# Layer 1 of a two-layer mixer: modulation sums rest until a row pass ends, one norm and the first attention scores come one unit later

## The chip, the core and the metric

The kernel runs on one NeuronCore of a Trainium2 chip, as one launch. The metric is device time in microseconds (us), the median of repeated runs. A NeuronCore has engines that each work through their own list of instructions: TensorE (PE in the profile) multiplies, ScalarE (ACT) applies functions and copies, VectorE (DVE) does elementwise work and sums, GpSimd (POOL) does a small power function here, and SyncE (SP) issues the loads.

## The reference, cut to what matters

Two layers act on 256 latent and 256 context tokens of width 2048, in float32. Each layer is

```
shift, scale, gate = split(silu(c) @ w_mod + b_mod)
h    = rms_norm(x) * (1 + scale) + shift
u, v_sgu, za, q, k, v, zb = split(h @ w_in)        # D_IN = 5632
attn = softmax(rope(norm(q)) . rope(norm(k))) . v  # 8 heads of 128, 2 key/value heads
sgu  = gelu(u) * (w_sgu . norm(gelu(v_sgu)) + b_sgu)
x    = x + gate * (concat(sgu * silu(za), attn * silu(zb)) @ w_out)
```

In layer 1, the last one, the context gives only keys and values, so that q, u, v_sgu, za and zb are computed for 256 tokens and the 8 heads have two blocks of 128 queries each: 16 score blocks against 512 keys.

## The kernel before, in words

Every float32 operand is split into a high part `hi` and a rest `lo`, and a product is three matmuls: hi.hi, hi.lo, lo.hi (`three`, lines 334 to 336).

Most weights come through a `Stream`. The weights of a *job* (512 columns, for example "U0" or "ZA0") are eight *pieces* of 256 rows. For a piece, SP loads `raw`, ACT writes `hi` (line 200) and DVE writes `lo` (line 203). Three buffers hold `hi` and three hold `lo`; when the matmuls of piece n are about to be written down, the split of piece n+2 is written down first, and it takes the buffers that piece n-1 leaves. A piece of layer 1 is two *units* of twelve matmuls with 256 columns (six with 512 columns in jobs of kind "tok"). A job collects in four PSUM tiles of a ring of four (`acc`; two in "tok" jobs); after the last piece ACT applies gelu or silu to each (`act`, line 640, or `s`, line 663), which frees the tile for the next job.

The order on PE, SP, DVE and ACT is the order in which the Python program writes instructions down. After each unit the program calls `tick()`, which lets every waiting generator task advance if its countdown is over. So a `yield n` in a task means "n units later", and moving a task by one unit moves its instructions past whatever else is written down in that unit, on every engine. The tasks that matter here are:

- `next_task` prepares layer 1's rows: `hm` (DVE, line 722), `h` high (ACT, line 723), `h` rest (DVE, line 724) for 16 slices, first for latents, then for context. It sets `hold[0]`, and while that is set `mod_task` waits.
- `mod_task` computes modulation vectors on DVE, one `junk` instruction at a time (line 278, 128x1024).
- `sgu_v` evaluates gelu on a tile (line 663) and starts `head_norm`, whose first step is four sums of squares on ACT (`sq`, line 436).
- `attention_task` works through the heads. For head j: at its first step the scores `s` (PE), their maximum `nmx` (DVE, line 529) and the exponentials `p` (ACT, line 532); one unit later, on PE, the values `o` and the query transposes `qt` (each every second head) and the transposes `tp` of the head before; two units later the evacuations `qT` and `pt` (ACT line 470, then DVE line 471), a reciprocal (DVE, line 631) and the scaling of `p` (ACT, line 632); then, one unit later, the next head. In layer 1 that is four units, or two pieces, per head, called a *round* below.

Of the kernel before, what the change touches and what calls it, by code (L numbers as in the profile page):

```python
# [40 lines left out]
REST = (2, 0)  # L41
SGU_LAG = {4: 15, 2: 6}
CTX_WAIT = (15, 15)
HOLD_KT = 14
PAIRED = 2
NEXT_PACE = (1, 2)
MIX_LAG = 3
# [2 lines left out]
SGU_GAP = {4: 2, 2: 3}  # L50
# [12 lines left out]
def mixer_kernel(ctx: ExitStack, tc: tile.TileContext, a, out):  # L63
# [23 lines left out]
    def big(shape, dt=F32, s="big"):  # L87
        return u8.tile(shape, dt, tag="u8", name=nm(s))
# [4 lines left out]
    def misc(s="ms"):  # L93
        return msp.tile([P, 512], F32, tag="ms", name=nm(s))
# [4 lines left out]
    def small(shape, tag, dt=F32, bufs=None):  # L99
        kw = {} if bufs is None else {"bufs": bufs}  # L100
        return sp.tile(shape, dt, tag=tag, name=nm(tag), **kw)

    def t2(shape, s, dt=F32):
        return sp.tile(shape, dt, tag="t2", name=nm(s), bufs=NT2)

    def view(ap, pat, **kw):
        return ap.rearrange(pat, **kw)
# [197 lines left out]
    def spawn(gen, wait=0):  # L305
        tasks.append([gen, wait])
# [69 lines left out]
    hold = [False]  # L376
# [44 lines left out]
    def rstd_of(ss, n, mean_n):  # L421
        r = small([P, 4], "rs", bufs=12)[:, :n]
        V.tensor_scalar(out=r, in0=ss, scalar1=1.0 / mean_n, scalar2=EPS, op0=ALU.mult, op1=ALU.add)  # L423
        G.tensor_tensor(out=r, in0=r, in1=nhalf[:, :n], op=ALU.pow)  # L424
        return r

    def bc_last(ap, n, w):
        return view(ap, "p (h o) -> p h o", o=1).broadcast_to([P, n, w])

    def head_norm(q, n, kind):  # L430

        sq = t2([P, 512], "sq")[:, :n * HD]
        ss = small([P, 4], "ss", bufs=12)[:, :n]
        if kind in ACT_SUM:
            for h in range(n):
                S.activation(sq[:, h * HD:(h + 1) * HD], q[:, h, :], AF.Square, accum_out=ss[:, h:h + 1])
            yield NORM_PACE[0]
        else:
            S.activation(view(sq, "p (h d) -> p h d", h=n), q, AF.Square)
            yield NORM_PACE[0]  # L440
            V.tensor_reduce(out=ss, in_=view(sq, "p (h d) -> p h d", h=n), axis=AX.X, op=ALU.add)
        r = rstd_of(ss, n, HD)
        yield NORM_PACE[1]
        if kind in ACT_NORM:
            for h in range(n):
                S.activation(q[:, h, :], q[:, h, :], AF.Copy, scale=r[:, h:h + 1])
        else:
            V.tensor_tensor(out=q, in0=q, in1=bc_last(r, n, HD), op=ALU.mult)
# [20 lines left out]
    def evac_split(hi, lo, ps):  # L469
        S.copy(hi, ps)  # L470
        V.tensor_tensor(out=lo, in0=ps, in1=hi.bitcast(F32), op=ALU.subtract)

    def attention_task(L, kv, qa, units, done):
# [87 lines left out]
        rest = REST[L["l"]]  # L561
# [2 lines left out]
        ps, qT = turn_queries(*pairs[0])  # L564
        yield 1
        evac_split(qT[0], qT[1], view(ps[:, :256], "p (h d) -> p h d", h=2))
        yield rest + 1
        hold[0] = False
        paces = HEAD_PACE[L["l"]]
        n = len(heads)  # L570
# [88 lines left out]
    def sgu_v(L, buf, hf, nt):  # L659

        def f(tt, ps):
            b = buf[:, tt]
            S.activation(b, view(ps, "p (g d) -> p g d", g=4), AF.Gelu_apprx_tanh)  # L663
            spawn(head_norm(b, 4, "s"), SGU_GAP[nt] * tt)
        return f

    def sgu_consts(l, hf):
# [27 lines left out]
    def rows_diag(p1, nt):  # L695
        r = rstd_of(p1[:, :nt], nt, D)
        dg = t2([P, 512], "dg")
        for t in range(nt):
            V.tensor_scalar(out=dg[:, t * P:(t + 1) * P], in0=ident, scalar1=r[:, t:t + 1], scalar2=None,
                            op0=ALU.mult)  # L700
        return dg

    def rows_bc(dg, nt):
        pb = misc("rsb")
        for t in range(nt):
            ts = slice(t * P, (t + 1) * P)
            T.matmul(pb[:, ts], ones, dg[:, ts], start=True, stop=True)
        return pb[:, :nt * P]
# [9 lines left out]
    def modulate(L, kt, stream, xs, rb, hi, lo):  # L718

        sl = slice(stream, stream + 1)  # L720
        t_ = t2([P, 512], "hm")[:, :xs.shape[-1]]
        V.scalar_tensor_tensor(out=t_, in0=xs, scalar=L["A"][:, kt, sl], in1=rb, op0=ALU.mult, op1=ALU.mult)
        S.activation(hi, t_, AF.Identity, bias=L["B"][:, kt, sl])  # L723
        return lambda: V.scalar_tensor_tensor(out=lo, in0=t_, scalar=L["B"][:, kt, sl], in1=hi.bitcast(F32),
                                              op0=ALU.add, op1=ALU.subtract)
# [188 lines left out]
    def run_groups():  # L914
        first_pair()
        for gi in range(2, len(GROUPS)):
# [3 lines left out]
            for u in range(3 * NT):  # L920
                if u in LOADS:
                    load_w(p + 1, LOADS.index(u))
                if nxt and u in WAVE[0]:
                    mod_step(gi + 1, WAVE[0].index(u))
                if nxt and u == WAVE[1]:
                    nxt.finish()
                    make = rows_h(gi + 1)
                if make and u >= WAVE[2]:
                    make.pop(0)()
                if u in MOD_LOADS:  # L930
                    mod_load(gi + 2, MOD_LOADS.index(u) // 2)
                if u in SPLITS:
                    i = SPLITS.index(u)
                    split_w(p + (i > 0), (2, 0, 1)[i])
                if not nxt:
                    if u == 1:
                        st.load_to(4)
                    if u in (5, 9):
                        st.split_to(u // 4)
                    if u == ATT_AT:  # L940
                        spawn(attention_task(L0, kv0, qa0, [(hf, tt) for hf in range(2) for tt in range(NT)], done0))
                group_unit(p, *divmod(u, NT))
                tick()
# [68 lines left out]
    def sq_row(kt, s, xs):  # L1012
        later(0, lambda: later(0, add_square(sums1[0][:, s], xs, kt == 0)))
# [48 lines left out]
    def kv_post1():  # L1062
        q = qkv1["q"]
        spawn(attention_task(L1, qkv1["kv"], [q[:, 0], q[:, 1]], [(hf, tt) for hf in range(2) for tt in LAT], done1))
# [24 lines left out]
    def out_job1(cn):  # L1089
        def ev(fb, ps):  # L1090
# [6 lines left out]
    rest = [Job(w1, KV0, "tok", range(NT), lhs1,  # L1097
                                      lambda tt, ps: S.copy(qkv1["kv"][:, tt], ps), pre=kv_pre1, post=kv_post1)]
# [34 lines left out]
    def next_task(s):  # L1133

        if s:
            yield CTX_WAIT[1]
            for fb in range(4):
                sq_row(12 + fb, s, rows1[fb])
                yield 1
        hold[0] = True  # L1140
        yield 3
        p1 = misc("rs1")
        for t in range(NLAT):
            T.matmul(p1[:, t:t + 1], sums1[0][:, s, t * P:(t + 1) * P], ones[:, 0:1], start=True, stop=True)
        yield 1
        dg = rows_diag(p1, NLAT)
        yield 1
        if s == 0:
            rb1.append(small([P, 512], "rb", bufs=1))
        rb = rb1[0][:, s * SEQ:(s + 1) * SEQ]  # L1150
        S.copy(rb, rows_bc(dg, NLAT))
        hs = [None] * 4
        rest = lambda: None
        for kt in range(KT):
            if kt % 8 == 0:
                hs[kt // 8] = big([P, 8, SEQ], F32R, s="h1")
                hs[2 + kt // 8] = big([P, 8, SEQ], F32R, s="h1")
            assert ("mod", D) in emitted
            nxt = modulate(L1, kt, s, x1[s][kt // 8][:, kt % 8, :], rb, hs[kt // 8][:, kt % 8, :],
                           hs[2 + kt // 8][:, kt % 8, :])  # L1160
            rest()
            rest = nxt
            if kt > 1:
                hold[0] = kt < HOLD_KT
                h1[s] = hs
                yield NEXT_PACE[s]
        rest()
    rb1 = []

    both = ((0, LATS), (1, CTXS))  # L1170
# [7 lines left out]
    for fb in (0, 2):  # L1178
        for n in held:
            last_unit(n, 0, LATS, (fb, fb + 1))  # L1180
        for f_ in (fb, fb + 1):
            sq_row(12 + f_, 0, last_rows(0, f_))
    spawn(next_task(0))
    rows1 = []
    for n in held[:-TAIL]:
        st.ahead(n)
        last_unit(n, 1, CTXS)
    for fb in (0, 2):
        for n in held[-TAIL:]:
            if fb:  # L1190
                st.ahead(n)
            last_unit(n, 1, CTXS, (fb, fb + 1))
        later(CTX_WAIT[0], lambda fb=fb: rows1.extend(last_rows(1, f_) for f_ in (fb, fb + 1)))
    spawn(next_task(1))
    while h1[0] is None:
        tick()
# [65 lines left out]
```

## Time and profile before

| | us |
|---|---|
| median of 3 runs | 1189.98 (1189.29 to 1190.85) |
| the profiled execution's own time | 1189.5 |
| its span, first to last instruction | 1187.7 |
| PE busy | 1162.2 (98% of the span) |
| DVE busy | 873.3 (74%) |
| ACT busy | 522.3 (44%) |

The granted PE clock is 1.00 throughout. The chain of work that ended last is PE for 90% of the span. Layer 1's rows are computed from about 779 us on, its attention runs from about 887 to 1036 us, beside the jobs U0, ZA0, the second SGU job, U1 and part of ZA1. Matmuls overlap, so the distance from one start to the next shows what PE achieves, and the duration of one is longer than that.

### The profile page before, as it was taken

To read this page: it belongs to the slowest core of one execution; us is meant where nothing else is said; L and a number is where in the kernel's file an instruction comes from. 1 tells how busy PE (TensorE), PEld (TensorE's weight loads), DVE (VectorE), ACT (ScalarE), POOL (GpSimd) and SP (SyncE) were. 2 spreads that over 40 slices of the span, in tenths; PEclk is the share of its full clock that TensorE was granted. 3 is DMA by queue.
4 is the path that set the end of the run, shared out by engine and by line. 5 is a ranking of instruction groups with operands and counts; after the bars stand their busy time and mean duration, and the time that the engine had idled before them with its cause. 6 is when DMAs were issued, how large, how long until landed. Compare 5 with 4: busy or idle time off the path is not lost.

```text
span 1187.7 us, 17503 instructions
## 1 busy us (share of the span) xinstructions
PE 1162.2 (98%) x6624; PEld 989.7 (83%) x6624; DVE 873.3 (74%) x1485; ACT 522.3 (44%) x992; POOL 47.6 (4%) x47
## 2 busy tenths in 40 slices
PE   4899999999999999999999999999999999999998
PEld 2567678888888888888888888987888989999998
DVE  5567769656675679789987999878657777676444
ACT  5423225565555433242232223156366777555332
POOL 0000002011000000010100000000011001000000
PEclk9999999999999999999999999999999999999999
DMA  9987772433343456777876766837466667687552
GB/s 321 385 304 283 259 255 76 154 106 108 107 117 97 145 189 234 236 222 242 295 265 229 247 211 232 280 112 263 138 197 195 205 205 227 198 280 235 197 194 90
DMA packets 114661, 247.49 MB, mean 208 GB/s; under 512 B 8544, under 2 KB 19328, under 8 KB 113808
## 3 DMA queue, kind: packets, MB, share of 16 engines
q1 hardware_dynamic: 112960, 242.03, 62.3%
q0 software_dynamic: 1184, 4.29, 1.1%
q8 instruction: 52, 0.85, 0.3%
q14 instruction: 33, 0.27, 0.1%
q10 hardware_dynamic: 432, 0.05, 0.0%
HBM read 244.23 MB, written 2.11 MB: 207 GB/s over the span
## 4 chain that ended last, share of the span: by engine, by line
PE 90%; DVE 4%; ACT 3%; issue 1%; DMA 1%; POOL 0%; SPq 0%; DVEq 0%; POOLq 0%; ACTq 0%
PE acc L334 27%; PE acc L335 27%; PE acc L336 27%; PE mod L232 2%; PE tp L539 1%; DVE lo L203 1%; PE sg L689 1%; ACT hi L200 1%; PE s L336 1%; DMA mod<-in_w_mod 1%; PE o L336 1%; PE o L335 1%; PE o L334 1%; PE s L335 1%; PE s L334 1%
## 5 line engine op out<-in xcount | busy, mean ns | idle before, releaser
L200 ACT CAST hi<-raw 128x1024 fp32r<-128x1024 f32 x236 | 246.9, 1046 | 381.0 <-PE acc L335 263.4
L203 DVE TENSOR_TENSOR lo<-raw,hi 128x1024 fp32r<-128x1024 f32 x236 | 288.0, 1222 | 129.8 <-ACT hi L200 129.3
L278 DVE SCALAR_TENSOR_TENSOR junk<-raw,scb 128x1024 f32<-128x1024 f32 x224 | 273.1, 1219 | 17.9 <-DMA raw<-in_w_modt 10.1
L334 PE MATMUL acc<-hh,hi 128*128 128x512 f32 x384 | 152.6, 397 | 0.0
L336 PE MATMUL acc<-hh,lo 128*128 128x512 f32 x384 | 149.8, 390 | 0.0
L335 PE MATMUL acc<-hl,hi 128*128 128x512 f32 x384 | 149.7, 390 | 0.0
L334 PE MATMUL acc<-hi,hh 128*128 128x512 f32 x320 | 129.3, 404 | 4.6 <-ACT hh L723 3.9
L335 PE MATMUL acc<-lo,hh 128*128 128x512 f32 x320 | 125.9, 393 | 1.0 <-DVE lo L808 1.0
L336 PE MATMUL acc<-hi,hl 128*128 128x512 f32 x320 | 125.9, 393 | 0.1
L334 PE MATMUL acc<-h,hi 128*128 128x256 f32 x384 | 110.3, 287 | 1.0 <-ACT s L663 1.0
L336 PE MATMUL acc<-h,lo 128*128 128x256 f32 x384 | 108.6, 283 | 0.0
L335 PE MATMUL acc<-h,hi 128*128 128x256 f32 x384 | 108.5, 283 | 0.0
L334 PE MATMUL acc<-mh,hi 128*128 128x512 f32 (+1 forms) x304 | 106.5, 350 | 0.0
L336 PE MATMUL acc<-mh,lo 128*128 128x512 f32 (+1 forms) x304 | 106.4, 350 | 0.0
L335 PE MATMUL acc<-ml,hi 128*128 128x512 f32 (+1 forms) x304 | 106.4, 350 | 0.0
L334 PEld LDWEIGHTS acc<-hi,hh 128*128 128x128 f32 x320 | 60.6, 189 | 30.1 <-issue 6.6
L336 PEld LDWEIGHTS acc<-hh,lo 128*128 128x128 f32 x384 | 72.1, 188 | 15.4
L335 PEld LDWEIGHTS acc<-hl,hi 128*128 128x128 f32 x384 | 72.3, 188 | 13.5
L334 PEld LDWEIGHTS acc<-hh,hi 128*128 128x128 f32 x384 | 72.2, 188 | 13.4
L424 POOL TENSOR_TENSOR rs<-rs,nhalf 128x4 f32<-128x4 f32 (+1 forms) x36 | 42.0, 1167 | 887.8 <-DVE rs L423 887.8
L335 PE MATMUL acc<-lo,h 128*128 128x512 f32 x192 | 75.3, 392 | 1.2 <-DVE lo L203 0.8
L334 PE MATMUL acc<-hi,h 128*128 128x512 f32 x192 | 75.7, 394 | 0.0
(165 smaller groups left out, 2144.0 us busy)
## 6 DMA issues: line engine op xcount, KB each, us to landing
raw<-in_w_in SPq DMA_DIRECT2D x173, 512.0 KB, 4.4
raw<-in_w_modt SPq DMA_DIRECT2D x128, 512.0 KB, 4.9
raw<-in_w_out SPq DMA_DIRECT2D x64, 512.0 KB, 4.9
mod<-in_w_mod SPq DMA_DIRECT2D x15, 1024.0 KB, 9.0
raw<-in_w_mod SPq DMA_DIRECT2D x30, 512.0 KB, 9.8
scb<-crow SPq DMA_DIRECT2D x6, 1024.0 KB, 7.9
xT<-in_xT SPq DMA_DIRECT2D x8, 512.0 KB, 8.0
x<-in_xT POOLq DMA_DIRECT2D x4, 1024.0 KB, 11.2
```

Source lines behind the costliest of these rows:

```text
L200: S.copy(hi, rs)
L203: V.tensor_tensor(out=lo, in0=rs, in1=hi.bitcast(F32), op=ALU.subtract)
L232: T.matmul(self.ps[j:j + 32, :wd], sc[:, k, :], self.raw[k], start=k < 4, stop=k >= KT - 4)
L278: V.scalar_tensor_tensor(out=junk, in0=rs[i], scalar=1.0, in1=scb[:, :, s_, :], op0=ALU.mult, op1=ALU.mult, accum_out=part[:, g, s_, q:q + 1])
L334: T.matmul(ps, lhi, rhi, start=first, stop=False)
L335: T.matmul(ps, lhi, rlo, start=False, stop=False)
L336: T.matmul(ps, llo, rhi, start=False, stop=last)
L424: G.tensor_tensor(out=r, in0=r, in1=nhalf[:, :n], op=ALU.pow)
L539: T.transpose(out=tp[:, c * P:(c + 1) * P], in_=p_[:, c * P:(c + 1) * P], identity=ident)
L689: T.matmul(ps[:, tt * P:(tt + 1) * P], buf[:, tt, g, :], ws[:, g, :], start=True, stop=True)
```

## The change

Three edits, all for layer 1. `next_task` no longer clears `hold[0]` at slice 14 of its 16 slices but after the last. `attention_task` yields 2 instead of 1 before the first scores where `REST` is 0, which is layer 1. `sgu_v` starts the norm of an SGU job's first tile one unit later where a job has two tiles, which is layer 1.

```diff
-HOLD_KT = 14
...
         evac_split(qT[0], qT[1], view(ps[:, :256], "p (h d) -> p h d", h=2))
-        yield rest + 1
+        yield rest + 1 if rest else 2
         hold[0] = False
...
             S.activation(b, view(ps, "p (g d) -> p g d", g=4), AF.Gelu_apprx_tanh)
-            spawn(head_norm(b, 4, "s"), SGU_GAP[nt] * tt)
+            spawn(head_norm(b, 4, "s"), SGU_GAP[nt] * tt if tt or nt > 2 else 1)
...
             if kt > 1:
-                hold[0] = kt < HOLD_KT
                 h1[s] = hs
                 yield NEXT_PACE[s]
         rest()
+        hold[0] = False
```

No instruction is added or taken away; the order changes. Line numbers after the change are one lower than before. The two texts below are DVE's list in job U0 of layer 1, from the evacuation of the second query pair to the next but one round. `lo` is a piece's rest, `junk` a modulation sum, `nmx` the maximum of a head's scores, `act` the gelu of U0's results. Before:

```order
L471 TENSOR_TENSOR qT_7820<-qt_7817,qT_7820 128x256
L471 TENSOR_TENSOR pt_7821<-tp_7822,pt_7821 128x4x128
L631 RECIPROCAL sm_7798<-sm_7798 128x1
L278 SCALAR_TENSOR_TENSOR junk_6441,mpart_6440<-raw_7332,scb_6448 128x1024
L529 TENSOR_REDUCE nmx_7892<-s_7888 128x1
L203 TENSOR_TENSOR lo_7869<-raw_7737,hi_7868 128x1024
L203 TENSOR_TENSOR lo_7916<-raw_7776,hi_7915 128x1024
L645 TENSOR_TENSOR s_1320_7347<-s_1320_7347,act_7926 128x2x128
```

Of the change:

```order
L470 TENSOR_TENSOR qT_7835<-qt_7832,qT_7835 128x256
L470 TENSOR_TENSOR pt_7836<-tp_7837,pt_7836 128x4x128
L630 RECIPROCAL sm_7809<-sm_7809 128x1
L202 TENSOR_TENSOR lo_7857<-raw_7731,hi_7856 128x1024
L277 SCALAR_TENSOR_TENSOR junk_6441,mpart_6440<-raw_7333,scb_6448 128x1024
L528 TENSOR_REDUCE nmx_7899<-s_7895 128x1
L202 TENSOR_TENSOR lo_7905<-raw_7768,hi_7904 128x1024
L644 TENSOR_TENSOR s_1318_7341<-s_1318_7341,act_7915 128x2x128
```

One of the round's two `lo` now stands between the evacuations and the maximum `nmx`; before, both stood behind it. The next two texts are ACT's list at the end of job U0, from the exponentials on; `acc` are U0's PSUM tiles. Before:

```order
L532 ACTIVATE p_7894,sm_7895<-s_7888,nmx_7892 128x512
L200 CAST hi_7915<-raw_7776 128x1024
L640 ACT_TABLE_LOAD
L640 ACTIVATE act_7926<-acc_7609 128x256
L640 ACTIVATE act_7934<-acc_7616 128x256
L640 ACTIVATE act_7945<-acc_7630 128x256
L640 ACTIVATE act_7953<-acc_7637 128x256
L470 CAST pt_7821<-tp_7910 128x4x128
L632 ACTIVATE p_7894<-p_7894,sm_7895 128x512
L200 CAST hi_7963<-raw_7834 128x1024
L532 ACT_TABLE_LOAD
```

Of the change:

```order
L531 ACTIVATE p_7901,sm_7902<-s_7895,nmx_7899 128x512
L199 CAST hi_7904<-raw_7768 128x1024
L639 ACT_TABLE_LOAD
L639 ACTIVATE act_7915<-acc_7600 128x256
L639 ACTIVATE act_7923<-acc_7607 128x256
L639 ACTIVATE act_7939<-acc_7623 128x256
L639 ACTIVATE act_7947<-acc_7630 128x256
L199 CAST hi_7951<-raw_7818 128x1024
L469 CAST pt_7836<-tp_7925 128x4x128
L631 ACTIVATE p_7901<-p_7901,sm_7902 128x512
L531 ACT_TABLE_LOAD
```

The gelu of U0 still stands behind the exponentials, one `hi` and a table load; the second `hi` of the round now stands ahead of the `pt` evacuation. On PE the scores `s` of this head stand one unit later: between them and the first matmul of the next job there were three units and a `tp`, and there are now two units and a `tp`.

## Rows read from the trace of the kernel before

**Rows 1.** Page, part 1: busy time, share of the span, instructions.

```profile
PE 1162.2 (98%) x6624; PEld 989.7 (83%) x6624; DVE 873.3 (74%) x1485; ACT 522.3 (44%) x992; POOL 47.6 (4%) x47
```

**Rows 2.** PE's waits: us in total, times, longest us.

```profile
PE s L336 <- DVE qT L471: 1.5, 2, 1.0
PE acc L334 <- ACT s L663: 1.0, 1, 1.0
...
PE acc L335 <- DVE lo L203: 0.8, 1, 0.8
```

**Rows 3.** Timeline, end of layer 1's latent rows: start, us, instruction, idle before.

```profile
800.24 1.22 DVE L278 SCALAR_TENSOR_TENSOR junk<-raw,scb 128x1024 f32<-128x1024 f32 x1
800.38 1.04 ACT L200 CAST hi<-raw 128x1024 fp32r<-128x1024 f32 x1
...
802.18 1.22 DVE L203 TENSOR_TENSOR lo<-raw,hi 128x1024 fp32r<-128x1024 f32 x1
```

**Rows 4.** Timeline of PE at the first SGU tiles and the first scores.

```profile
897.17 0.28 PE L336 MATMUL acc<-h,lo 128*128 128x256 f32 x1
898.44 0.39 PE L334 MATMUL acc<-h,hi 128*128 128x256 f32 x1 [0.98 <-ACT s L663]
...
904.01 0.40 PE L335 MATMUL s<-kT,qT 128*128 128x512 f32 x1
904.92 0.50 PE L336 MATMUL s<-kT,qT 128*128 128x512 f32 x1 [0.52 <-DVE qT L471]
```

**Rows 5.** Timeline of ACT at the first SGU tiles.

```profile
896.63 0.30 ACT L436 ACTIVATE sq<-s 128x128 f32<-128x128 f32 x1
...
897.80 0.58 ACT L663 ACTIVATE s<-acc 128x512 f32<-128x512 f32 x1
```

**Rows 6.** Timeline of ACT and DVE, one round and the end of U0.

```profile
914.54 1.05 ACT L200 CAST hi<-raw 128x1024 fp32r<-128x1024 f32 x1 [0.24 <-PE acc L335]
...
915.49 0.37 ACT L470 CAST qT<-qt 128x256 fp32r<-128x256 f32 x1
915.76 0.59 ACT L470 CAST pt<-tp 128x512 fp32r<-128x512 f32 x1
...
916.16 1.22 DVE L203 TENSOR_TENSOR lo<-raw,hi 128x1024 fp32r<-128x1024 f32 x1
917.30 0.42 DVE L471 TENSOR_TENSOR qT<-qt,qT 128x256 fp32r<-128x256 f32 x1
917.63 0.68 DVE L471 TENSOR_TENSOR pt<-tp,pt 128x512 fp32r<-128x512 f32 x1
...
918.30 1.21 DVE L278 SCALAR_TENSOR_TENSOR junk<-raw,scb 128x1024 f32<-128x1024 f32 x1
...
920.77 0.69 DVE L529 TENSOR_REDUCE nmx<-s 128x1 f32<-128x512 f32 x1 [1.26 <-PE s L336]
...
921.50 0.69 ACT L532 ACTIVATE p<-s,nmx 128x512 f32<-128x512 f32 x1 [1.36 <-DVE nmx L529]
...
922.18 1.04 ACT L200 CAST hi<-raw 128x1024 fp32r<-128x1024 f32 x1
923.23 1.28 ACT L640 ACT_TABLE_LOAD   x1
...
924.52 1.37 ACT L640 ACTIVATE act<-acc 128x256 f32<-128x256 f32 x4
```

**Rows 7.** Timeline of PE, scores of three heads and the next job's first matmul.

```profile
919.87 0.40 PE L334 MATMUL s<-kT,qT 128*128 128x512 f32 x1
...
925.31 0.28 PE L334 MATMUL acc<-h,hi 128*128 128x256 f32 x1
...
926.75 0.40 PE L334 MATMUL s<-kT,qT 128*128 128x512 f32 x1
...
935.28 0.40 PE L334 MATMUL s<-kT,qT 128*128 128x512 f32 x1
```

## The prediction

> **What bounds the kernel now.** I read the page first: PE is busy for 98% of the span [rows 1], so time can only be won where PE stands still, and any new stop of PE is time lost. The view of PE's waits comes next, because it names the few stops. Three of them lie in layer 1 [rows 2]: once for a `lo` (0.8 us), once for the gelu of an SGU tile (1.0 us), and for the `qT` of the first scores. Then I read the timeline around each, and that of one round of the attention with the end of job U0. Everywhere else in layer 1 matmul follows matmul without a stop, so the three edits aim at the three stops, and the most they can win together is about 2.6 us. Whether they win it depends on what the shift does to the rest of the attention, which today runs without any stop.
>
> **Edit 1, modulation rests.** DVE starts a `junk` at 800.24, ahead of the `lo` that PE waits for. That `lo` starts at 802.18, though its `hi` was started at 800.38 and took 1.04 [rows 3]. Without the `junk` the `lo` can start when the `hi` is done, at about 801.45: 0.73 us earlier, and PE goes on 0.73 earlier. The remaining 0.1 or so of that stop stays. The `junk` moves behind the last slice, where the next `lo` is not yet wanted. At the end of the context rows PE does not wait at all, so the same edit is worth nothing there. Gain 0.73.
>
> **Edit 2, the norm of the first SGU tile.** PE starts at 897.17 and again at 898.44, where the regular distance of these matmuls is 0.12: a stop of 1.15 us for the gelu of the second tile [rows 4]. On ACT that gelu stands behind four `sq`, which take from 896.63 to 897.80, 1.17 us [rows 5]. With the norm one unit later the gelu comes first, and starts 1.17 earlier. Gain 1.15. The four `sq` then run behind it. The norm of this tile is wanted much later, so this costs nothing by itself.
>
> **Edit 3, the first scores.** PE stops before the third score matmul: 904.01 to 904.92, where 0.23 is regular, so 0.68 [rows 4]. One more unit ahead of the scores is worth 1.44 us (one unit runs from 925.31 to 926.75 [rows 7]). But PE now arrives 1.15 earlier because of edit 2, while the chain that makes `qT` has not moved. So 0.68 + 1.15 - 1.44 = 0.39 of the stop is left; gain 0.29. The three gains together are 0.73 + 1.15 + 0.29 = 2.17 us.
>
> **What edit 3 moves besides.** Every later step of the attention is one unit later too, and a round is four units or two pieces long. So the whole attention shifts by half a piece against the splits `hi` and `lo`, in all 16 heads. Nothing new is executed, no transfer grows, and SP's loads only change places among themselves; but two orders matter.
>
> *On DVE*, one `lo` now stands ahead of `junk` and `nmx`. *On ACT*, the `hi` that goes with it now stands ahead of `qT` and `pt`. This `hi` cannot start before PE has left the buffer, that is, when PE starts a piece; row 914.54 shows such a start, released by PE. From there a chain runs through both engines, each link start to start [rows 6]: `hi` to `qT` 0.95 (914.54 to 915.49), `qT` to `pt` 0.27, `pt` on ACT to `pt` on DVE 0.59 (the duration of row 915.76), `pt` to the next DVE work past the reciprocal 0.67 (917.63 to 918.30), the `lo` 1.14 (916.16 to 917.30), the `junk` 1.14 (the same size as a `lo`), `nmx` to the exponentials 0.73 (920.77 to 921.50), these to the other `hi` 0.68, and that `hi` 1.05 until ACT is free again (922.18 to 923.23). The sum is 7.22 us, and only then can the next round's `hi` start. In rounds without a `qT` an `o` copy takes its place, which I count as equal. Before the change the chain was short: `nmx` had no `lo` ahead of it and waited 1.26 us for PE [rows 6].
>
> PE's own time for a round is 6.88 or 8.53 us, alternating (919.87, 926.75, 935.28 [rows 7]), 15.41 for two. So the chain would just keep up, with 0.5 us per round to spare, if nothing else were on ACT.
>
> **What this costs at the first job end.** At the end of U0, ACT loads the gelu table and runs four `act`, and the next job's first matmul needs the PSUM tile of the first. Before: scores start at 919.87, `act` at 924.52, so its tile is free at about 924.9 (one of four in 1.37 us, with a little for the signal), and PE wants it at 925.31: 0.4 us to spare [rows 6, 7]. After: from the piece start, 7.22 to the table load, 1.29 for the load (923.23 to 924.52), 0.4 for the first `act`, 8.91 in all. PE wants the tile after its short round, 6.88. PE stops for 2.0 us.
>
> A bound from below: even if `nmx` followed the scores as closely as it does now, the tile would be free 924.9 - 919.87 = 5.05 after the scores start, and PE, with one unit less between, would want it 5.44 - 1.44 = 4.0 after. So 1.05 us is the least, and it comes from PE's order alone.
>
> **What it costs at the later ones.** After a job end the chain carries more than four plain rounds until the next: four rounds are 28.9; the gelu or silu table load 1.29; four `act` 1.3 (ACT cannot go on to the next `hi` before them); the reload of the table for the exponentials, which also stands in the chain, 1.29; and four `sq` of a later query block, 1.17, by row 896.63 [rows 5]. That is 33.95. PE's four rounds are 30.82 [rows 7]. The difference, 3.1 us, is what PE must wait in every such stretch: part of it while the chain is late within the rounds, most of it at the job end. There are three stretches: to the end of ZA0, of the second SGU job, and of U1. The SGU job has two gelu in place of four `act`, a missing `junk` in one round and, against that, four copies of finished gates; I take the same 3.1. Three stretches are 9.4 us.
>
> Here the Trainium skill bears on a price. Its page "ScalarE: Activation LUTs", section "What ACT_TABLE_LOAD costs", gives about 2.66 us for each switch of table set, of which 1.28 is the load and the rest a drain. The row agrees with the load (1.28) and shows no gap between it and the first `act`; by the page's full price each of seven loads in the chain would cost 1.4 more, which as an estimate would end near 1209.
>
> **The sum.** The profiled execution took 1189.5, its span 1187.7. 1189.5 - 2.17 + 2.0 + 9.4 = 1198.7. The median of the runs was 0.5 above the profiled execution, so I predict 1199.
>
> Two costs are not in the sum. In the SGU stage the score, transpose and SGU products share a ring of four PSUM tiles, and the third SGU product's reader on DVE now also stands behind `junk` and `nmx`; between 0 and 1 us, taken as 0. The norm of a later query block on DVE (`qa`) stands in the chain of two rounds, and gate copies in one; together 0 to 4 us, taken as 0 against the missing `junk`. These set the high end.
>
> **The rivals.**
> - *The chain catches up* in every stretch, so that each job end pays its own 2.0 and nothing is carried on. For it: 0.5 us per round to spare, and PE's stop gives the chain time. Against it: the extra work of a stretch is 5.05 us and the spare 1.9. Four ends: 1190 - 2.2 + 8.0 = 1195.8; 1193.8 if the SGU job's end does not wait. Chance 0.20.
> - *Only PE's order counts*: `nmx` is not late, and three ends pay 1.05. It decides if the `hi` that opens the chain is started well before PE's piece start. 1190 - 2.2 + 3.2 = 1191. Against it: row 914.54 is released by PE. Chance 0.10.
> - *Faster*: all three stops vanish and the job ends still fit, 1190 - (0.73 + 1.15 + 0.68) = 1187.4. The place that decides is the first matmul of ZA0: it must find its tile 1.44 us earlier than now relative to the scores, where 0.4 is to spare. It would take an order on ACT in which the gelu passes the exponentials, and the list shows none. Chance 0.08.
>
> **Chances and range.** My forecast, with the missing and the extra links of the chain as its own range, 1197 to 1204, has 0.60; 0.02 is left for anything worse. What a measurement of this kernel can tell from no change is about 0.2%, 2.4 us. Faster by more than that holds 0.08, within it 0.10 (the second rival), slower 0.82. The range from 1193.5 to 1205 takes in the first rival and the uncounted costs and leaves out the other two.
>
> **What would show it.** Right: PE's waits list a new line "acc <- ACT act" with two or three stops of 2 to 4 us at about 925, 958 and 1022 us, and one for the gelu `s` near 990; DVE's `nmx` no longer waits for PE but follows a `junk`; PE busy stays near 1162 while the span grows; the wait for `lo` near 802 falls to a few tenths, the wait for `s` near 898 is gone. The prediction is wrong if `nmx` still starts within 1 us of the scores, or if the first matmul of ZA0 does not wait. It is too high if the stops after the first are all 2 us or less.

## The result and the profile after

| | before | after |
|---|---|---|
| median | 1189.9 us (1189.29 to 1190.85, 4 runs) | 1202.62 us (1202.02 to 1205.29, 4 runs) |
| the profiled execution, its span | 1189.5, 1187.7 | 1202.96, 1201.2 |

The ratio is 1.011, interval 1.0098 to 1.0122: slower by 12.7 us, where 1199 with 1193.5 to 1205 was predicted. The page's first part, which answers to [rows 1]:

```profile
PE 1168.3 (97%) x6624; PEld 992.7 (83%) x6624; DVE 873.1 (73%) x1485; ACT 521.8 (43%) x992; POOL 47.7 (4%) x47
```

The number of instructions is unchanged, and DVE and ACT are as busy as before. PE is busy 6 us longer for the same matmuls, which the prediction had excluded; about half of that is the lower clock shown further down. PE's waits after the change (us, times, longest us), to be read against [rows 2]:

```profile
PE acc L333 <- ACT act L639: 6.8, 3, 2.7
...
PE acc L333 <- ACT s L662: 1.7, 1, 1.7
PE s L335 <- DVE qT L470: 1.3, 2, 0.9
...
PE tp L538 <- DVE s L680: 0.5, 1, 0.5
...
PE s L333 <- ACT qT L469: 0.3, 1, 0.3
```

The wait for the `lo` near 802 is gone from the list, and that for the gelu near 898 too. The first line is new: three job ends, at U0, ZA0 and U1. The second is the end of the second SGU job, near 996. The timeline of PE shows the three ends after U0's:

```profile
962.29 0.80 PE L333 MATMUL acc<-hi,h 128*128 128x512 f32 x1 [2.66 <-ACT act L639]
...
997.44 0.38 PE L333 MATMUL acc<-h,hi 128*128 128x256 f32 x1 [1.67 <-ACT s L662]
...
1031.66 0.39 PE L333 MATMUL acc<-h,hi 128*128 128x256 f32 x1 [2.05 <-ACT act L639]
```

The timeline of the round that ends U0, engine by engine, answers to [rows 6]:

```profile
918.12 1.05 ACT L199 CAST hi<-raw 128x1024 fp32r<-128x1024 f32 x1 [0.81 <-ACT hi L199]
919.07 0.37 ACT L469 CAST qT<-qt 128x256 fp32r<-128x256 f32 x1
919.33 0.59 ACT L469 CAST pt<-tp 128x512 fp32r<-128x512 f32 x1
...
923.62 0.69 ACT L531 ACTIVATE p<-s,nmx 128x512 f32<-128x512 f32 x1 [2.08 <-DVE nmx L528]
...
924.30 1.03 ACT L199 CAST hi<-raw 128x1024 fp32r<-128x1024 f32 x1
925.35 1.28 ACT L639 ACT_TABLE_LOAD   x1
926.64 1.32 ACT L639 ACTIVATE act<-acc 128x256 f32<-128x256 f32 x4
...
920.63 1.21 DVE L202 TENSOR_TENSOR lo<-raw,hi 128x1024 fp32r<-128x1024 f32 x1
921.76 1.22 DVE L277 SCALAR_TENSOR_TENSOR junk<-raw,scb 128x1024 f32<-128x1024 f32 x1
...
922.90 0.68 DVE L528 TENSOR_REDUCE nmx<-s 128x1 f32<-128x512 f32 x1
...
920.87 0.40 PE L333 MATMUL s<-kT,qT 128*128 128x512 f32 x1
...
924.75 0.28 PE L335 MATMUL acc<-h,lo 128*128 128x256 f32 x1
927.08 0.39 PE L333 MATMUL acc<-h,hi 128*128 128x256 f32 x1 [2.05 <-ACT act L639]
```

Read it down: `nmx` now follows a `lo` and a `junk` without a gap, where before it had waited 1.26 us for PE. From the `hi` at 918.12 to the first `act` are 8.52 us, and 0.44 more to PE: 8.96, for which the prediction had 8.91. PE, which reached the job's end at 924.87, stands still until 927.08. That is a cost of 2.21 us, counted from start to start less the regular distance, as all costs of stops below; the 2.05 in the bracket is PE's idle time, which begins with the end of the matmul before.

The view of windows (us; busy time and instructions of PE, PEld, DVE, ACT, POOL; then the granted clock, the DMA share and GB/s) shows what was not foreseen:

```profile
926.00:928.00 2.00, 0.92 (x7) 0.92 (x8) 1.53 (x4) 1.99 (x6) 0.00 (x0) 0.95 0.55 170
928.00:930.00 2.00, 2.00 (x11) 2.00 (x11) 1.08 (x3) 1.39 (x2) 0.00 (x0) 0.50 0.69 235
...
962.00:964.00 2.00, 1.71 (x4) 1.42 (x5) 1.48 (x5) 2.00 (x5) 0.00 (x0) 0.50 0.45 90
...
996.00:998.00 2.00, 0.56 (x4) 0.56 (x5) 0.99 (x1) 1.99 (x5) 0.00 (x0) 1.00 0.95 363
...
1030.00:1032.00 2.00, 0.34 (x2) 0.34 (x3) 1.53 (x3) 1.99 (x4) 0.00 (x0) 1.00 0.62 230
```

After two of the four stops the granted clock is 0.50, the 1.2 GHz level, and PE multiplies at about half the rate. From 927.95 to 931.32 the starts of sixteen matmuls lie 0.21 us apart instead of 0.12, which costs 1.45 us; from 962.29 to 965.41 seven with 512 columns lie 0.43 to 0.59 apart instead of 0.23, which costs 1.5. After the stops that end at 997.44 and 1031.66 the clock stays at 1.00.

To add it all up, take every distance from one matmul's start to the next over the median distance for its shape (0.12 us with 256 columns, 0.227 with 512). Between 750 and 1200 us this excess is about 4.8 us before and 17.4 after: 12.6 of the 13.5 by which the two spans differ.

| term | predicted, us | measured, us |
|---|---|---|
| edit 1, the `lo` near 802 | -0.73 | -0.68 (0.97 to 0.29) |
| edit 2, the gelu near 898 | -1.15 | -1.15 (gone) |
| edit 3, the first scores | -0.29 | -0.18 (0.68 to 0.50) |
| first job end | +2.0 | +2.21 |
| three later job ends | +9.4 | +7.33 (2.82; 0.48 and 1.82; 2.21) |
| the ring of four PSUM tiles | 0, bound 1 | +0.65 (a `tp` at 916.10) |
| lower clock | not thought of | +2.95 |
| distances of a few tenths | 0 | +1.4 (the difference) |

### The profile page after: what moved, and what is told of

Read it like the earlier page. It is cut to its first block, busy times and chain, and to the rows that moved or that the text cites. A ratio compares the mean times of both kernels' runs of the same rounds, so it can differ in the third digit from the quotient of the medians.

```text
span 1201.2 us, 17524 instructions
## 1 busy us (share of the span) xinstructions
PE 1168.3 (97%) x6624; PEld 992.7 (83%) x6624; DVE 873.1 (73%) x1485; ACT 521.8 (43%) x992; POOL 47.7 (4%) x47
## 4 chain that ended last, share of the span: by engine, by line
PE 82%; DVE 7%; ACT 4%; issue 3%; DMA 3%; POOL 0%; SPq 0%; DVEq 0%; ACTq 0%; POOLq 0%
PE acc L333 24%; PE acc L334 24%; PE acc L335 24%; PE mod L231 2%; DVE lo L202 2%; DMA raw<-in_w_modt 2%; ACT hi L199 2%; PE tp L538 1%; DVE junk L277 1%; PE sg L688 1%; DMA mod<-in_w_mod 1%; PE s L335 1%; PE o L334 1%; PE o L335 1%; PE o L333 1%
## 5 line engine op out<-in xcount | busy, mean ns | idle before, releaser
L334 PEld LDWEIGHTS acc<-hl,hi 128*128 128x128 f32 x384 | 72.3, 188 | 13.5
L333 PEld LDWEIGHTS acc<-h,hi 128*128 128x128 f32 x384 | 74.2, 193 | 6.9 <-ACT act L639 4.5
```

Of the source, the lines that this page charges most:

```text
L333: T.matmul(ps, lhi, rhi, start=first, stop=False)
L334: T.matmul(ps, lhi, rlo, start=False, stop=False)
```

## The experiments

The theory (A): edit 3 alone makes the loss. It puts a `lo` ahead of `junk` and `nmx` on DVE and a `hi` ahead of `qT` on ACT; the exponentials get late, and with them the `act` that frees the PSUM tile at each job end. There are three rivals. The loss needs edit 1 or 2. The chain catches up everywhere. Only PE's own order counts, one unit less between scores and job end. The Trainium skill's page "ScalarE: Activation LUTs", section "What ACT_TABLE_LOAD costs", has a fourth, a price of about 2.66 us for every switch of table set. The expectations below give rivals letters of their own.

**Edit 3 alone, and edits 1 and 2 alone.** The first kernel is the one before with this line, the second is the one after without it:

```diff
-        yield rest + 1
+        yield rest + 1 if rest else 2
```

> Only the edit on the scores: first scores one unit later, the rest as before. Theory A (the shift of the attention by half a piece closes a chain over DVE and ACT and makes the job ends late): all of the loss is here; four job-end stops of 2 to 3 us stay, the gelu stop near 897 stays at 1.15, the stop before the first scores goes: 1202 to 1204.5. Rival B (the loss comes from the modulation sums being pushed into the attention): this kernel is within 1 us of before, 1189 to 1191.

Measured: 1206.64 (1204.73 to 1209.29, 4 runs; ratio 1.0143, interval 1.0129 to 1.0156). The job ends stop PE for 2.21, 3.30, 2.97 (in two parts) and 2.22 us; the stops of edits 1 and 2 are there (0.99 and 1.14), that of the first scores is gone. The median is about 2 us above the upper end of what I expected. The ends of ZA0 and of the SGU job cost 1.2 us more than in the changed kernel, and the windows show a third fall of the clock:

```profile
926.00:928.00 2.00, 0.91 (x8) 0.71 (x6) 0.75 (x1) 1.98 (x4) 0.00 (x0) 1.00 0.91 318
928.00:930.00 2.00, 1.04 (x8) 1.04 (x9) 1.53 (x5) 1.99 (x6) 0.00 (x0) 1.00 0.42 109
...
964.00:966.00 2.00, 2.00 (x6) 1.51 (x6) 1.07 (x3) 1.47 (x3) 0.00 (x0) 0.50 0.85 254
...
1000.00:1002.00 2.00, 2.00 (x9) 1.71 (x8) 1.05 (x3) 1.17 (x3) 0.38 (x1) 0.54 0.16 59
...
1034.00:1036.00 2.00, 2.00 (x12) 2.00 (x12) 1.20 (x4) 2.00 (x5) 0.00 (x0) 0.57 0.71 204
```

Here the clock falls after the second, third and fourth job end, and not after the first, though that stop is as long as in the changed kernel (2.05 us idle in both). The mean granted clock of the four executions is 0.996, 0.994, 0.992 and 0.992, and their times rise in this order: 1204.73, 1206.45, 1206.82 and 1209.29 us. The four of the changed kernel had 0.994 to 0.998, and the one at 0.994 was the longest, 1205.29.

> The edits on the modulation sums and on the norm, without the one on the scores. Theory A: no stop at any job end; the lo stop near 802 falls from 0.97 to 0.3 and the gelu stop is gone, but the stop before the first scores grows from 0.68 to about 1.8 because the chain of qT has not moved, so PE wins only the 0.7 of the lo: 1189.2 (1188.7 to 1190). Rival B: 1200 or more.

Measured: 1189.92 (1188.66 to 1191.12, 11 runs; ratio 0.9998, interval 0.9989 to 1.0007), and no job end stops PE. The `lo` stop is 0.27 and the gelu stop gone, 1.8 us won; but PE now arrives earlier at the first scores and idles 1.78 us there (a cost of 1.95), where [rows 4] had 0.52. The timeline and the windows behind it:

```profile
905.10 0.50 PE L335 MATMUL s<-kT,qT 128*128 128x512 f32 x1 [1.78 <-DVE qT L470]
```

```profile
906.00:908.00 2.00, 2.00 (x11) 2.00 (x11) 2.00 (x3) 0.78 (x2) 0.27 (x1) 0.50 0.79 256
908.00:910.00 2.00, 2.00 (x15) 2.00 (x15) 1.06 (x2) 1.04 (x1) 0.00 (x0) 0.77 0.33 46
```

The longer stop takes 1.3 us back, and the lower clock behind it (distances of 0.21 from 905.58 to 908.78) another 1.4 in this execution. It is not so in all: five executions with a mean granted clock of 1.00 took 1188.66 to 1189.29 us, the other six, with 0.997 or 0.998, took 1189.92 to 1191.12.

So edit 3 alone makes the loss, and edits 1 and 2 alone change nothing that their median shows. The expectations' B is out.

**One link less: the `lo` behind `junk` and `nmx`.** All three edits, and once layer 1's scores have begun each `lo` of the stream is written down one unit later:

```diff
-            later(0, rest)
+            later(1 if attending[0] and late[0] else 0, rest)
...
+    late = [False]
...
         hold[0] = False
+        late[0] = L["l"] == 1
```

> All three edits, and during layer 1's attention each piece's lo is written down one unit later, so that on DVE it stands behind junk and nmx again; ACT's order and PE's order are those of the change. Theory A: the chain loses its 1.14 us link, 6.1 a round, so it keeps up with PE and carries nothing from one job end to the next; each job end then pays what is left of 2.2, about 1.1, which is also PE's own part: 1190 to 1193.5. Rival C (it is ACT's hi ahead of qT and pt that counts, DVE's lo is hidden): 1201 to 1203, stops as before. Rival D (PE's order costs nothing once DVE is repaired): 1187.5 to 1188.5, no stop at a job end.

Measured: 1193.06 (1192.77 to 1194.4, 6 runs; ratio 1.0027, interval 1.0016 to 1.0038). The same round in its timeline:

```profile
918.11 1.05 ACT L199 CAST hi<-raw 128x1024 fp32r<-128x1024 f32 x1 [1.44 <-PE acc L335]
...
920.62 1.21 DVE L277 SCALAR_TENSOR_TENSOR junk<-raw,scb 128x1024 f32<-128x1024 f32 x1
920.86 0.40 PE L334 MATMUL s<-kT,qT 128*128 128x512 f32 x1
...
921.76 0.69 DVE L529 TENSOR_REDUCE nmx<-s 128x1 f32<-128x512 f32 x1
...
925.95 0.39 PE L334 MATMUL acc<-h,hi 128*128 128x256 f32 x1 [0.93 <-ACT act L641]
```

The `hi` that opens the chain starts at the same time as after the change, released by PE as the prediction had read it from [rows 6]. `nmx` starts 1.14 earlier, one DVE instruction, and PE 1.13 earlier. It now follows the scores by 0.90, as closely as before the change (919.87 to 920.77 [rows 6, 7]). The job ends cost 1.09, 1.68 and 1.10 us, and that of the SGU job nothing. The first and the third are what the prediction gave as the bound from PE's order alone, 1.05: this part of the rival on PE's order is real, and stays when the chain is shortened. The expectation's C is out, since the stops fell though ACT's `hi` kept its place, and D is out, since three stops are left. The clock keeps 1.00, and the 2.95 us are gone with the long stops.

**The whole attention a full round later.** All three edits, with the scores of layer 1 three units later still, which makes four against the kernel before. A round is four units, so that against the splits everything stands as before the change:

```diff
-        yield rest + 1 if rest else 2
+        yield rest + 1 if rest else 5
```

> All three edits, but the first scores come a whole round (four units) later instead of one unit, so that the attention meets the pieces as it did before. Theory A: it is the half-piece shift that costs, not lateness: no stop at a job end, none before the first scores, gelu stop gone: 1187 to 1188.5. Rival E (later scores as such cost, since the attention then ends later than the gates that need it): above 1190, with new stops after 1030.

Measured: 1188.86 (1188.34 to 1190.54, 11 runs; ratio 0.9995, interval 0.9986 to 1.0004). No job end stops PE, and `nmx` again waits for PE and stands ahead of the `lo`:

```profile
918.27 0.69 DVE L528 TENSOR_REDUCE nmx<-s 128x1 f32<-128x512 f32 x1 [1.99 <-PE s L335]
918.88 1.22 DVE L202 TENSOR_TENSOR lo<-raw,hi 128x1024 fp32r<-128x1024 f32 x1
```

It is not lateness of the scores that costs, but their place within the round. The time is 0.4 above the expected range; two small stops are new, told below with the best version.

**The other link: no `junk` beside the heads.** All three edits; layer 1's modulation sums rest until the attention is over and run at half the spacing elsewhere, so that they are done in time:

```diff
-MOD_PACE = (1.3, 1.3, 1.6)
+MOD_PACE = (1.3, 1.3, 0.8)
...
                     attending[0] = hf != units[-1][0]
+                    if not attending[0]:
+                        hold[0] = False
...
-        hold[0] = False
+        hold[0] = L["l"] == 1
```

> All three edits, and the modulation sums (junk) rest during the whole attention of layer 1 and run closer together behind it; lo stays ahead of nmx. Theory A (the length of the chain counts, whichever link is taken out): the chain loses 1.14 us, as with lo moved behind, so the stops at the job ends fall to 1.1 to 1.7 us each and the time to 1190.5 to 1194. Rival F (it is the lo itself, waiting for its hi, that holds up nmx, and the junk only fills a gap): stops stay at 2.2 to 2.8 and the time at 1201 to 1203.

Measured: 1208.68 (1206.68 to 1211.64, 4 runs; ratio 1.0161, interval 1.0144 to 1.0177). As a time this missed by 15 us. Where the link was taken out it did what was expected, and F is out: the job ends cost 1.09, 1.68, 0.86 and 1.09. The loss is elsewhere, before and behind the attention: 2.0 us at 813, 1.4 in two stops at 882 and 895, and 10.6 between 1070 and 1130, the largest of them here:

```profile
1106.03 1.22 DVE L277 SCALAR_TENSOR_TENSOR junk<-raw,scb 128x1024 f32<-128x1024 f32 x1 [2.72 <-DMA raw<-in_w_modt]
...
1107.18 1.22 DVE L202 TENSOR_TENSOR lo<-raw,hi 128x1024 fp32r<-128x1024 f32 x1
...
1108.45 0.58 PE L335 MATMUL acc<-h,lo 128*128 128x256 f32 x1 [2.90 <-DVE lo L202]
```

A `junk` waits 2.72 us for its transfer, behind it on DVE stands a `lo`, and PE waits for the `lo`. The granted clock falls behind this stop too, and stays low for longer than after any job end:

```profile
1108.00:1110.00 2.00, 1.55 (x7) 1.55 (x8) 1.74 (x4) 0.71 (x2) 0.00 (x0) 0.50 0.81 251
...
1112.00:1114.00 2.00, 2.00 (x12) 2.00 (x11) 1.33 (x3) 0.83 (x3) 0.00 (x0) 0.50 0.94 359
```

That is about 2.8 of the 10.6 us. I had counted the moved sums as hidden and not asked what their loads do when they are packed. So this kernel bears out the link by its job ends, and its time measures something else.

**No table loads.** All three edits, with gelu and silu of layer 1's gates and SGU tiles replaced by the identity, so it computes something else; ACT's instructions stay, their table loads go.

```diff
-            S.activation(b, view(ps, "p (g d) -> p g d", g=4), AF.Gelu_apprx_tanh)
+            S.activation(b, view(ps, "p (g d) -> p g d", g=4), AF.Gelu_apprx_tanh if nt > 2 else AF.Identity)
...
-    rest += [gate_job1(ZB0 + 512 * hf, SILU, lambda hf=hf: qkv1["q"][:, hf], 2 + hf) for hf in range(2)]
+    rest += [gate_job1(ZB0 + 512 * hf, ONE, lambda hf=hf: qkv1["q"][:, hf], 2 + hf) for hf in range(2)]
```

(U0, U1, ZA0 and ZA1 are changed like the last line.)

> All three edits; in layer 1 the gelu and silu of the gates and of the SGU tiles are replaced by the identity, so that no table load stands in the attention any more (another function is computed, the instructions are the same). Theory A with a load priced at 1.29 us, as the trace has it: the first job end's stop falls from 2.2 to 0.9, each of the later stretches loses two loads, 2.6 us, and keeps 0.6 or so: 1190.5 to 1193.5. If a load cost 2.66 us, the figure for a switch of table set in the Trainium skill's page "ScalarE: Activation LUTs", the stop at the first job end would be gone, and the later ones too: 1188 to 1189.5. Rival G (loads are hidden, the order alone counts): 1201 or more.

Measured: 1193.86 (1193.62 to 1195.61, 6 runs; ratio 1.0033, interval 1.0021 to 1.0045). The job ends cost 0.80, 1.46, 0.43 and 0.79, each 1.36 to 1.42 less than after the change, and the clock does not fall behind any of them. The time is 0.4 above the expected range: the later ends were expected to lose two loads each and lost the price of one, so the reload for the exponentials is not in what an end pays. Two stops ahead of scores in the SGU stage, 0.53 and 0.74, come on top, where the changed kernel has one of 0.48. ACT and PE at the end of U0:

```profile
924.57 1.03 ACT L199 CAST hi<-raw 128x1024 fp32r<-128x1024 f32 x1
925.50 0.93 ACT L639 ACTIVATE act<-acc 128x256 f32<-128x256 f32 x3
...
925.94 0.38 PE L333 MATMUL acc<-h,hi 128*128 128x256 f32 x1 [0.64 <-ACT act L639]
```

From the `hi` to the first `act` there are 0.93 us here and 2.34 with the load (924.30 to 926.64): a table switch costs 1.41 in this chain, the load's 1.28 and 0.13 more; without the load the first `act` starts 0.10 before the `hi` has ended. The Trainium skill's page "ScalarE: Activation LUTs", section "What ACT_TABLE_LOAD costs", states 2.66; here the measurement decides.

**Best version found.** The round-later kernel leaves two small stops, for a `lo` (0.39) and for `s` (0.77) near 904 to 906, the second for the norm of an SGU tile. One more unit of lag for the SGU products:

```diff
-SGU_LAG = {4: 15, 2: 6}
+SGU_LAG = {4: 15, 2: 7}
```

> The three edits with the first scores a whole round later, and besides the SGU products of layer 1 one unit later (lag 7 in place of 6), because PE then waits 0.77 for the second tile's norm. Theory A: that stop goes and nothing else changes: 1187.5 to 1188.5, 0.3 to 0.8 below the kernel a round later alone. Rival: the products one unit later push the gates' sums, the time does not change: 1188.9.

Measured: 1187.93 (1187.36 to 1190.5, 11 runs; ratio 0.9987, interval 0.9978 to 0.9995). The stop for `s` is gone, and no job end stops PE. By the ratio it beats the kernel before by about 1.5 us; that is small, but its interval leaves out 1. It takes nearly 15 us less than the changed kernel.

## Why the prediction was right, and where it was not

**Right: which edit decides, and through what.** Each edit removed its stop nearly to the size read from the rows, and edit 3's shift of the order cost several times more. The chain across ACT and DVE was 8.96 us long where 8.91 had been worked out, and taking a link out, the `lo`, the `junk` or the table load, shortened the first job end by 1.12, 1.12 and 1.41. "PE stops for 2.0 us" at the first end holds (2.21 measured: the chain's 8.96 less the 6.75 from the `hi` at 918.12 to 924.87, for which the prediction had taken 6.88). That the chain "would just keep up" in plain rounds holds too: ACT idles 0.81 ahead of that `hi`. Of the signs named ahead, the new waits, `nmx` behind `junk`, and the two vanished stops came true; "PE busy stays near 1162" did not.

**A job end taken apart.** In the first end 1.09 of the 2.21 us is PE's order (it stays when `lo` or `junk` leaves the chain) and 1.12 is one DVE instruction of 1.14 too many ahead of `nmx`.

**The step that was mis-sized: "the difference, 3.1 us, is what PE must wait in every such stretch".** Measured were 2.82, 2.30 and 2.21, together 7.33 instead of 9.4. At U1's end PE idles 2.05 us, exactly as at U0's, and the `hi` that opens its last round stands 2.75 ahead of the scores, as at U0's end (918.12 to 920.87). So nothing is carried on from job to job there, and in this kernel the rival in which the chain catches up (2.0 at each of four ends, 8.0 in all) described the mechanism better than the forecast: measured 9.54 for all four, between its 8.0 and the forecast's 11.4. Only ZA0's end is 0.61 more, and the row for that is on DVE: behind the reciprocal of that round, and ahead of its `lo`, stands a `qa` of a later query block from 955.23 to 955.82. The rows of the rounds that end ZA0 and U1:

```profile
952.72 1.05 ACT L199 CAST hi<-raw 128x1024 fp32r<-128x1024 f32 x1
...
955.23 0.67 DVE L447 TENSOR_TENSOR qa<-qa,rs 128x512 f32<-128x512 f32 x1
955.47 0.40 PE L333 MATMUL s<-kT,qT 128*128 128x512 f32 x1
...
1022.70 1.05 ACT L199 CAST hi<-raw 128x1024 fp32r<-128x1024 f32 x1 [0.90 <-ACT qa L552]
...
1025.45 0.40 PE L333 MATMUL s<-kT,qT 128*128 128x512 f32 x1
```

This 0.59 is the cost that the prediction named and took as 0. About the same 0.6 stands between these two ends in three experiments (1.68 against 1.09 twice, 1.46 against 0.80).

With edit 3 alone the two ends are 1.09 apart (3.30 against 2.21), and there the forecast's carry does show. The round that ends ZA0 in that kernel:

```profile
953.34 0.35 ACT L553 COPY qa<-o 128x256 f32<-128x256 f32 x1
953.60 1.05 ACT L200 CAST hi<-raw 128x1024 fp32r<-128x1024 f32 x1
...
955.87 0.40 PE L334 MATMUL s<-kT,qT 128*128 128x512 f32 x1
```

The opening `hi` stands without a gap behind a copy on ACT, 2.27 ahead of the scores instead of 2.75: the chain is 0.48 late. In that execution the clock had not fallen behind U0's end. In the changed kernel it had, PE lost 1.45 us by it, and the chain had that much more time to catch up. So the two errors of the forecast, the carry and the clock, are not independent; this is argued from two profiles, and no run sets the clock by itself.

**What made up for it.** The 2.1 us too much for the later ends makes up for most of the 2.95 too little for the clock; the 0.65 of the `tp`, the small rest and the sizes of the single terms are left. Taken away by itself, the lower clock would leave a result near 1199.7, and somewhat more if ZA0's end then became longer, as with edit 3 alone. That the forecast is 3.6 from the median is partly luck.

**Open.** What decides after which stop the clock falls: it did after idle times of 2.05 and 2.66 us in one profile, and in the same profile not after 1.67 and 2.05; with edits 1 and 2 alone it did after 1.78. I tried nothing on it by itself. The 1.4 us of small distances were not traced one by one.

## What to carry to other kernels

When work is shifted by part of a period against another periodic stream, list the order on every in-order engine at the new phase, and walk the chain through all of them until it closes on a buffer that the bound engine releases; compare its length to the bound engine's period and look at the place where a reader must free a tile. A shift by a whole period keeps the order, as the kernel moved by one round shows. Stops removed one at a time are worth little where the next wait is on the same chain: edits 1 and 2 won 1.8 us, met 1.3 of it again at the first scores, and in the execution that was profiled lost the rest to the clock behind the longer stop.

## What the runs showed of the hardware that was not expected

The granted clock of TensorE can fall to the 1.2 GHz level after a single stop of about 2 us in an otherwise full stretch, and PE then loses more by it: 1.45 us behind the stop of 2.21, 1.5 behind that of 2.82, 1.4 behind one of 1.95, and about 2.8 behind the one of 3.06 at 1108 in the kernel without `junk` beside the heads. It did so after two of the four long stops in the changed kernel, after three of four with edit 3 alone, and not always after the same ones. In the profiled executions of the kernels whose job ends cost 1.7 us or less it stayed at 1.00 around all of them. A stop's price is thus not only its length, and it differs between kernels, and between executions of one kernel, by which stop happens to be hit: with edits 1 and 2 alone the executions at a granted clock of 1.00 and those at 0.997 or 0.998 lie 1.5 us apart in the median.
